# Making the down projection's input factors on chip, from raw activations, instead of reading them ready-made from DRAM

## The chip, the cores and the metric

One Trainium2 chip, and one of its cores: TensorE (PE) multiplies 128x128 tiles, VectorE (DVE) and ScalarE (ACT) do elementwise work, GpSimd (POOL) a little of it, and SyncE (SP) issues the transfers between DRAM and the on-chip memory SBUF, which 16 DMA engines carry out. The metric is the time of one execution on the device in microseconds (us), the median of several runs.

## The reference

One layer of an encoder over 2048 positions with a width of 1024: a mixer of three head groups, and then a gated feed-forward network (FFN) with a convolution, each within normalisations, conditioned scales and a residual. Only the FFN matters here:

```
h  = rms_norm(x, g_pre_ffn) * (1 + sc_f) + sh_f
up = dwconv3(h @ w_up, conv_w, conv_b)         # w_up: 1024 x 5632, width-3 convolution over positions
gate, val = split(up, 2)
y  = (gelu(gate) * val) @ w_down               # w_down: 2816 x 1024
x  = x + gt_f * rms_norm(y, g_post_ffn)
```

All of it is float32.

## The kernel before

Channels lie on the 128 partitions and positions along the free dimension. Every large product is computed in float16 with a float32 sum: each operand is split into a high part (its float16 rounding) and a low part (the rest), and a product is three matmuls, high x high, low x high, high x low (`mm3`).

The two projections of the FFN also go by Strassen's scheme in Winograd's form: a product of two matrices of 2 x 2 blocks takes seven products of blocks and not eight, and each of the seven multiplies a sum or a difference of blocks, a *factor*, by another. The kernel numbers them 1 to 7. For the down projection the blocks of the activations are two neighbouring k-tiles of 128 channels (a = 2j, b = 2j + 1) by two halves of 512 positions; with b11, b12 the two halves of a, and b21, b22 those of b, the activation factors are: 1: b11; 5: t5 = b12 - b11; 6: t6 = b22 - t5; 3: b22; 7: b22 - b12; 2: b21; 4: b21 - t6. The weights have factors of their own, made in SBUF by `wcomb` and written to DRAM (`wdd`) by `down_weights` during the up projection.

The positions are worked through in two *halves* (`p` in the up projection, `nt` in the down projection): 0 is positions 0 to 1022 after the convolution and 1 the rest. The down projection wants 1024 positions in each, so position 1023 comes from `p` = 1: it is the last column of a 512 column block in half 0, and the column is kept in `self.gx`.

*Up projection* (`ffn`): for each half, 22 pairs of tiles (a gate and a value), each with seven products; `up_act` convolves, applies the gelu and multiplies, and writes the result, float32, to DRAM (`grd`). Both halves of the up projection come before the down projection.

*Factors* (`gcomb`, lines 1785 to 1815): one process for each half, and in each, eleven pairs j of k-tiles. It loads the two raw tiles (2 x 512 KB), makes four combinations with four subtractions on VectorE (`tt`, line 277), splits all of it in high (ScalarE, `act`, line 272) and low (VectorE, line 277), and stores seven factors of 256 KB to DRAM (`gd`). The one for half 0 follows the up projection of half 1, pair by pair (`f_up[1][2j]`). The one for half 1 follows the down projection of half 0: it waits for `f_down[j]`, which is set at every third step of that. Column 511 is left out in half 0; `gx_comb` makes it for all factors (`gxc`) when the last pair of the up projection is done.

*Down projection* (`down`, from line 1865): for each half, products in the order `ORDER` = 1, 5, 6, 3, 7, 2, 4, and for each six steps k of two pairs j (the sixth has one). A step is 4 output tiles x 2 pairs x 3 = 24 matmuls of 512 columns, and a product 132. In half 0 the first product is computed for 511 columns, and then for the one column from `gxc` with 132 further matmuls. `down_stream` (line 1845) feeds it: for each step it loads a tile of weight factors and a tile of activation factors, 512 KB each, up to `D_LEAD` = 7 steps ahead. `down_evac` brings a product's four PSUM banks to the output tiles Y and sums their squares; when an output half is complete, after product 7 and after product 4, `ffn_out` normalises it, adds the residual and stores it. Its normalisation needs a small float32 matmul with ones on TensorE.

*The order of the work.* Processes are Python generators. Each yields the engine it wants, a planned duration and an earliest time, and a planner (`Sched`) with its own clock for each engine takes the request that can start first, with priorities among equals; the order that results, and for each instruction its planned start as a priority, goes to the framework, which puts every engine's instructions into one fixed list, allots the tiles and sets the waits. At run time each engine goes through its list in order, so an instruction that waits holds up all that stands behind it on its engine. All transfers are issued on SP's queue (`dma`, line 267). A transfer of n bytes is planned as n / 340e3 us of the queue and 2 us until it has landed; an addition of n columns on VectorE as 0.07 + 0.00105 n, a copy on ScalarE as 0.2 + 0.00084 n, and each hands on 0.12 us later.

SBUF's working tiles are 50 slots of 4112 bytes a partition (`u`): a 512 KB tile of weights, of factors or of raw activations takes one.

Of the kernel before, what the change touches and what calls it, by code (L numbers as in the profile page):

```python
# [10 lines left out]
F16 = mybir.dt.float16  # L11
I32 = mybir.dt.int32
AF = mybir.ActivationFunctionType
ALU = mybir.AluOpType
# [57 lines left out]
W_LEAD, W_RAW, U_PAIRS, D_LEAD, TAIL = 3, 1, 4, 7, 2  # L72
# [130 lines left out]
class Builder:  # L203
# [1452 lines left out]
    def ffn(self):  # L1656
        A = self.A
        self.cwt, self.carry = self.const([P, 44, 4]), self.const([P, 44, 2])
        self.gx, self.gxc = self.const([P, 2, NFF]), self.const([P, 7, 11, 2], F16)
        self.gd, self.wdd = self.dt([7, 2, 11, P, 1024], F16), self.dt([7, 11, P, 1024], F16)  # L1660
# [4 lines left out]
        self.f_g = [[Fut() for _ in range(11)] for _ in range(2)]  # L1665
        self.f_gr, self.f_down = [[Fut() for _ in range(NFF)] for _ in range(2)], [Fut() for _ in range(11)]
        self.grd = self.dt([2, NFF, P, 1024], F32)
        for p in range(2):
            self.sc.spawn(self.gcomb(p), 4)
        self.f_up = [[Fut() for _ in range(NFF)] for _ in range(2)]  # L1670
        self.f_gx, self.f_wd = Fut(), [Fut() for _ in range(11)]
# [74 lines left out]
    def up_act(self, p, i, U, f, done, pairs):  # L1746
# [32 lines left out]
        if p and i == NFF - 1:  # L1779
            self.sc.spawn(self.gx_comb(t + 0.3))  # L1780
# [3 lines left out]

    def gcomb(self, p):


        n, v = 511 + p, lambda x: x.rearrange("p (a b) -> p a b", a=2)
        e = G_ADD
        for j in range(11):  # L1790
            if p == 0:
                t = yield ("w", self.f_up[1][2 * j])
            else:
                t = yield ("w", self.f_down[j])
            for i in (2 * j, 2 * j + 1):
                yield ("w", self.f_gr[p][i])
            a, b = self.u([2, n]), self.u([2, n])
            ta = yield from self.dma(max(t, self.f_gr[p][2 * j].t), a, v(self.grd[p, 2 * j, :, 0:2 * n]))
            tb = yield from self.dma(max(t, self.f_gr[p][2 * j + 1].t), b, v(self.grd[p, 2 * j + 1, :, 0:2 * n]))
            t12, t34 = self.u([2, n]), self.u([2, n])  # L1800
            o = [self.u([2, 2, 512], F16) for _ in range(4)]
            if p == 0:
                for x in o:
                    yield from self.mset(0, x[:, :, :, 511:512], 0.0, eng="G")
            t1 = yield from self.tt(ta, t12[:, 0], a[:, 1], a[:, 0], ALU.subtract, eng=e[0])
            t3 = yield from self.tt(max(ta, tb), t34[:, 0], b[:, 1], a[:, 1], ALU.subtract, eng=e[1])
            t2 = yield from self.tt(max(t1, tb), t12[:, 1], b[:, 1], t12[:, 0], ALU.subtract, eng=e[2])
            t4 = yield from self.tt(t2, t34[:, 1], b[:, 0], t12[:, 1], ALU.subtract, eng=e[3])
            w = 0.0
            for i, (t, src, rs) in enumerate(((ta, a[:, 0], (1,)), (tb, b, (2, 3)), (t2, t12, (5, 6)),  # L1810
                                              (max(t3, t4), t34, (7, 4)))):
                t = yield from self.split(t, o[i][:, :, :, 0:n], src)
                for c, r in enumerate(rs):
                    w = yield from self.dma(t, self.gd[r - 1, p, j].rearrange("p (x n) -> p x n", x=2), o[i][:, :, c])
            self.f_g[p][j].set(w)

    def gx_comb(self, t):

        v = self.gx.rearrange("p s (j a) -> p a s j", a=2)
        (b12, b11), (b22, b21) = [(v[:, a, 0], v[:, a, 1]) for a in range(2)]  # L1820
        d = self.const([P, 4, 11], name="gt")
        S = ALU.subtract
        t = yield from self.tt(t, d[:, 0], b12, b11, S)
        t = yield from self.tt(t, d[:, 1], b22, d[:, 0], S)
        t = yield from self.tt(t, d[:, 2], b22, b12, S)
        t = yield from self.tt(t, d[:, 3], b21, d[:, 1], S)
        for r, src in ((1, b11), (2, b21), (3, b22), (4, d[:, 3]), (5, d[:, 0]), (6, d[:, 1]), (7, d[:, 2])):
            hi, lo = self.gxc[:, r - 1, :, HI], self.gxc[:, r - 1, :, LO]
            t = yield from self.act(t, hi, src, AF.Copy)
            t = yield from self.tt(t, lo, src, hi, S)  # L1830
        self.f_gx.set(t)
# [13 lines left out]
    def down_stream(self, q, lead):  # L1845
        for nt in range(2):
            for r in self.ORDER:
                for k in range(6):
                    t = yield ("acq", lead, 1)
                    n = 2 if k < 5 else 1  # L1850
                    for j in range(2 * k, 2 * k + n):
                        t = max(t, (yield ("w", self.f_wd[j])), (yield ("w", self.f_g[nt][j])))
                    w, g = self.u([n, 2, 512], F16), self.u([n, 2, 512], F16)
                    v = lambda d: d[2 * k:2 * k + n].rearrange("j p (x n) -> p j x n", x=2)
                    yield from self.dma(t, w, v(self.wdd[r - 1]))
                    t = yield from self.dma(t, g, v(self.gd[r - 1, nt]))
                    if nt == 0 and r != self.ORDER[0]:
# [7 lines left out]
    def down(self):  # L1865
# [6 lines left out]
        for nt in range(2):  # L1872
# [6 lines left out]
            for r in self.ORDER:  # L1879
# [19 lines left out]
                for pi, (c0, c1) in enumerate(parts):  # L1899
# [3 lines left out]
                    for k in range(6):  # L1903
# [13 lines left out]
                        if wide == 512 and pi == len(parts) - 1:  # L1917
                            lead.give(t)
# [229 lines left out]
```

## Time and profile before

| | us |
|---|---|
| median of 3 runs | 2234.53 (2234.34 to 2235.89) |
| the profiled execution's own time | 2235.86 |
| its span, first to last instruction | 2234.1 |
| TensorE busy, in the span | 2004.5 (90%) |
| VectorE busy | 1596.0 (71%) |
| ScalarE busy | 984.2 (44%) |
| GpSimd busy | 266.9 (12%) |

Over the span the DMA engines moved 478.11 MB, 214 GB/s in the mean. In the trace, times are counted from the span's start. TensorE's busy time comes from modelled ends of pipelined matmuls, so the count of matmuls in a stretch is the surer measure of its speed. "Granted clock" is the share of TensorE's full clock that the throttle left it. A row of a group of instructions has: line, engine, operation, out<-in (`u` a slot, `c` a constant, `ps` a PSUM bank, `d` DRAM), shapes, count | busy us, mean ns of one | idle time of the engine just before them and what ended it. A row of the timeline has: start, length, engine, line, operation, names, shapes, count, and in brackets the idle time before.

### The profile page before, as it was taken

What the parts mean: (1) busy time and instruction counts of PE and PEld (TensorE: products, weight loads), DVE (VectorE), ACT (ScalarE), POOL (GpSimd) and SP (SyncE); (2) the same over time, 40 slices, a digit from 0 to 9 for tenths busy, and PEclk for the clock granted to TensorE, in tenths of its full rate; (3) what the DMA queues carried; (4) which work ended last, traced back from release to release, by engine and by line L of the source; (5) the groups of instructions that cost most, each with busy time, mean ns of one, the idle gap of its engine ahead of it and who ended that gap; (6) DMA issues with size and microseconds to landing.
All of it is one profiled execution on the core that took longest, in us unless ns stands there. A gap on an engine that the chain in (4) does not pass through costs nothing.

```text
span 2234.1 us, 28331 instructions
## 1 busy us (share of the span) xinstructions
PE 2004.5 (90%) x10252; PEld 1000.6 (45%) x10252; DVE 1596.0 (71%) x2455; ACT 984.2 (44%) x1657; POOL 266.9 (12%) x390
## 2 busy tenths in 40 slices
PE   6778777989998778998999999999999999975997
PEld 2335565545554335443444444444444444432445
DVE  8999999976665665889988875878887724362016
ACT  3623232436566665566655543555555422211001
POOL 0564554020000000000000000000000000020002
PEclk9899899999999888999999999999999999997999
DMA  9351134772825453336655557888887899989933
GB/s 368 110 175 60 44 104 148 250 252 67 287 100 150 138 191 103 127 128 254 235 190 195 186 207 274 286 296 295 281 297 265 291 323 336 346 285 320 375 110 108
DMA packets 263919, 478.11 MB, mean 214 GB/s; under 512 B 23266, under 2 KB 149475, under 8 KB 263779
## 3 DMA queue, kind: packets, MB, share of 16 engines
q1 hardware_dynamic: 263778, 476.31, 61.4%
q8 instruction: 80, 1.31, 0.2%
q14 instruction: 61, 0.49, 0.1%
HBM read 299.30 MB, written 175.35 MB: 212 GB/s over the span
## 4 chain that ended last, share of the span: by engine, by line
PE 58%; DVE 26%; ACT 5%; issue 4%; DMA 4%; SPq 2%; POOL 1%; DVEq 0%; POOLq 0%; ACTq 0%
PE ps L318 58%; DVE u L277 13%; DVE u L291 9%; ACT u L272 5%; DMA u<-d 2%; DVE u L302 2%; SPq L267 2%; DVE u L446 1%; POOL u L277 1%; DVE u L284 0%; DMA u<-w_up 0%; DVE u L410 0%; DVE u L1327 0%; DMA u<-x 0%; DMA u<-w_ada 0%
## 5 line engine op out<-in xcount | busy, mean ns | idle before, releaser
L318 PE MATMUL ps<-u,u 128*128 128x512 f16 (+10 forms) x9306 | 1917.5, 365 | 158.4 <-DMA u<-d 53.1
L318 PEld LDWEIGHTS <-u 128*128 128x128 f16 (+1 forms) x9466 | 875.1, 101 | 1075.4 <-issue 178.4
L272 ACT ACTIVATE u<-u 128x1024 f16<-128x1024 f32 (+10 forms) x487 | 405.1, 861 | 378.2 <-DMA u<-d 126.1
L277 DVE TENSOR_TENSOR u<-u,u 128x512 f32<-128x512 f32 (+10 forms) x618 | 502.5, 845 | 74.4 <-ACT u L272 37.2
L272 ACT ACTIVATE u<-ps 128x512 f32<-128x512 f32 (+6 forms) x511 | 276.0, 555 | 536.8 <-PE ps L318 514.9
L291 DVE SCALAR_TENSOR_TENSOR u<-ps,u 128x512 f32<-128x512 f32 (+3 forms) x231 | 151.9, 664 | 264.5 <-PE ps L318 227.5
L291 DVE SCALAR_TENSOR_TENSOR u<-u,c,u 128x1023 f32<-128x1023 f32 (+5 forms) x248 | 293.5, 1203 | 46.1 <-ACT u L272 42.0
L291 DVE SCALAR_TENSOR_TENSOR u<-u,u 128x1024 f16<-128x1024 f32 (+7 forms) x225 | 239.7, 1090 | 24.0 <-ACT u L272 21.7
L277 POOL TENSOR_TENSOR u<-u,u 128x288 f32<-128x288 f32 (+9 forms) x169 | 189.2, 1134 | 420.5 <-DVE u L291 255.9
L277 DVE TENSOR_TENSOR u<-u 128x512 f32<-128x512 f32 (+8 forms) x206 | 106.0, 525 | 118.5 <-DMA u<-d 75.0
L272 ACT ACTIVATE u<-u,c 128x1023 f32<-128x1023 f32 (+2 forms) x104 | 120.0, 1157 | 108.8 <-DVE u L291 102.9
L307 POOL MEMSET u<- 128x1 f32 (+1 forms) x132 | 13.4, 104 | 1156.9 <-PE ps L318 615.8
L272 ACT ACTIVATE u<-u,st 128x384 f32<-128x384 f32 (+3 forms) x192 | 108.7, 594 | 35.8 <-DVE st L284 20.1
L318 PEld LDWEIGHTS ps<-u,u 128*128 128x128 f32 (+1 forms) x532 | 93.7, 189 | 65.2 <-DVE u L277 36.5
L318 PE MATMUL ps<-u,c 128*128 128x32 f32 (+4 forms) x190 | 66.3, 456 | 40.2 <-DVE u L302 18.0
L318 PE MATMUL ps<-c,u 128*128 128x128 f16 (+2 forms) x700 | 65.2, 217 | 17.9 <-ACT u L272 11.4
L272 ACT ACTIVATE c<-u 128x2 f32<-128x2 f32 (+1 forms) x88 | 17.8, 202 | 124.6 <-DVE u L291 124.4
L1327 DVE CUSTOM_DVE_ANT_0 u<-ps,u 128x384 f32<-128x384 f32 (+1 forms) x96 | 49.2, 537 | 29.9 <-PE ps L318 29.2
L302 DVE TENSOR_TENSOR_SCAN u<-u,u 128x512 f32<-128x512 f32 (+1 forms) x72 | 68.8, 963 | 1.1 <-ACT u L272 0.9
L291 DVE SCALAR_TENSOR_TENSOR u<-u,st,u 128x384 f16<-128x384 f32 (+1 forms) x96 | 55.6, 607 | 11.9 <-ACT u L272 11.6
L318 PEld LDWEIGHTS ps<-u,c 128*128 128x128 f32 (+1 forms) x190 | 29.1, 176 | 73.1 <-issue 29.1
L277 DVE TENSOR_TENSOR u<-ps,u 128x512 f32<-128x512 f32 (+2 forms) x96 | 56.1, 603 | 5.6 <-PE ps L318 5.2
(58 smaller groups left out, 379.9 us busy)
## 6 DMA issues: line engine op xcount, KB each, us to landing
u<-d SPq DMA_DIRECT2D x298, 512.0 KB
d<-u SPq DMA_DIRECT2D x158, 512.0 KB
d<-u SPq DMA_DIRECT2D x265, 256.0 KB
u<-w_ada SPq DMA_DIRECT2D x48, 512.0 KB
u<-w_up SPq DMA_DIRECT2D x44, 512.0 KB
u<-d SPq DMA_DIRECT2D x76, 256.0 KB
u<-x SPq DMA_DIRECT2D x32, 512.0 KB
u<-d SPq DMA_DIRECT2D x26, 511.0 KB
```

Of the source, the lines that this page charges most:

```text
L267: self.SP.dma_start(out, in_)
L272: self.S.activation(out, in_, func, **kw)
L277: (self.V if eng == "V" else self.G).tensor_tensor(out, a, b, op)
L291: self.V.scalar_tensor_tensor(out, a, s, b, op0, op1)
L302: self.V.tensor_tensor_scan(out, d0, d1, 0.0, ALU.mult, ALU.add)
L307: (self.V if eng == "V" else self.G).memset(out, v)
L318: self.PE.matmul(o, a, b, start=st, stop=sp, skip_group_check=chain)
L446: V.tensor_tensor_reduce(out=w, in0=w, in1=self.crep, op0=ALU.mult, op1=ALU.add, scale=1.0, scalar=0.0, accum_out=mod[:, j:j + 1])
L1327: V.tensor_tensor_reduce(out=s_, in0=o, in1=self.bias[h // 2][:, h % 2, bo:bo + nk * 128], op0=ALU.add, op1=ALU.max, scale=1.0, scalar=-3e ...
```

## The change

`gcomb` and `gx_comb` are taken out, and with them the factors in DRAM (`gd`) and the column constants (`gxc`). `down_stream` now loads raw activations and makes the factors itself. In products 1, 5, 6 and 2 each step loads one raw block of two pairs, float32, 512 KB, into a slot (`load`: X1 = b11, X2 = b12, X3 = b22, X4 = b21); in half 0 the block has 511 columns from DRAM and its last by a small ScalarE copy out of `self.gx`. The combination is made in place by one subtraction over both pairs: product 5 turns X1 into X2 - X1, product 6 that into X3 - X1, product 7 turns X2 into X3 - X2, product 4 turns X1 into X4 - X1; products 3 and 2 take X3 and X4 as they are. So X1 lives from product 1 to product 4, X2 from 5 to 7, X3 from 6 to 7, X4 from 2 to 4. Then each step splits its factor in high (ScalarE) and low (VectorE). The first product of half 0 has all 512 columns, the one-column matmuls are gone, and `D_LEAD` is 6. The order of the seven products in `ORDER` stays as it was, and so do the weights' factors.

```diff
--- before.py
+++ after.py
@@ -69,7 +69,7 @@
 W_ON_V = 2
 N_SL = 3
 W_ADD, H_ADD, G_ADD, SSQ = "VVVV", "V", "VVVV", "V"
-W_LEAD, W_RAW, U_PAIRS, D_LEAD, TAIL = 3, 1, 4, 7, 2
+W_LEAD, W_RAW, U_PAIRS, D_LEAD, TAIL = 3, 1, 4, 6, 2
 F_GATE, H_GATE, D_FROM = 1, 1, (1, 0, 2)
 N_CH = 3
 N_PE = (1,)
@@ -1656,19 +1656,15 @@
     def ffn(self):
         A = self.A
         self.cwt, self.carry = self.const([P, 44, 4]), self.const([P, 44, 2])
-        self.gx, self.gxc = self.const([P, 2, NFF]), self.const([P, 7, 11, 2], F16)
-        self.gd, self.wdd = self.dt([7, 2, 11, P, 1024], F16), self.dt([7, 11, P, 1024], F16)
+        self.gx, self.wdd = self.const([P, 2, NFF]), self.dt([7, 11, P, 1024], F16)
         yield from self.dma(0, self.cwt, A["cw"])
         yield ("w", self.f_pc[F_GATE])
         wq, lead = [Fut() for _ in range(2 * NFF)], Sem(W_LEAD)
         self.sc.spawn(self.up_weights(wq, lead, Sem(W_RAW)))
-        self.f_g = [[Fut() for _ in range(11)] for _ in range(2)]
-        self.f_gr, self.f_down = [[Fut() for _ in range(NFF)] for _ in range(2)], [Fut() for _ in range(11)]
+        self.f_gr = [[Fut() for _ in range(NFF)] for _ in range(2)]
         self.grd = self.dt([2, NFF, P, 1024], F32)
-        for p in range(2):
-            self.sc.spawn(self.gcomb(p), 4)
         self.f_up = [[Fut() for _ in range(NFF)] for _ in range(2)]
-        self.f_gx, self.f_wd = Fut(), [Fut() for _ in range(11)]
+        self.f_wd = [Fut() for _ in range(11)]
         self.sc.spawn(self.down_weights(), 4)
         pairs = Sem(U_PAIRS)
         for p in range(2):
@@ -1776,59 +1772,9 @@
         t = yield from self.stt(max(t, tms[1]), g, g, SA, c[1][:, :NT], ALU.mult, ALU.mult)
         x = 1022 if p == 0 else 0
         yield from self.act(t, self.gx[:, p, i:i + 1], g[:, x:x + 1], AF.Copy)
-        if p and i == NFF - 1:
-            self.sc.spawn(self.gx_comb(t + 0.3))
         t = yield from self.dma(t, self.grd[p, i, :, 0:1022 + 2 * p], c[0][:, p:p + 1022 + 2 * p])
         pairs.give(t)
         done.set(t)
-    def gcomb(self, p):
...
-    def gx_comb(self, t):
...
 
     def down_weights(self):
@@ -1843,24 +1789,60 @@
     ORDER = (1, 5, 6, 3, 7, 2, 4)
 
     def down_stream(self, q, lead):
+        S = ALU.subtract
         for nt in range(2):
+            n = 511 + nt
+            X = {}
+            def load(x, k, ab, half):
+                i0, m = 4 * k + ab, 2 if k < 5 else 1
+                z = self.u([m, 512])
+                X[x, k] = z
+                t = 0.0
+                for i in range(i0, i0 + 2 * m, 2):
+                    for p in range(2):
+                        t = max(t, (yield ("w", self.f_gr[p][i])))
+                t = yield from self.dma(t, z[:, :, 0:n], self.grd[nt, i0:i0 + 2 * m - 1:2, :, half * n:half * n + n]
+                                        .rearrange("i p n -> p i n"))
+                if nt == 0:
+                    t1 = yield from self.act(0, z[:, :, 511], self.gx[:, 1 - half, i0:i0 + 2 * m - 1:2], AF.Copy)
+                    t = max(t, t1)
+                return t
             for r in self.ORDER:
                 for k in range(6):
                     t = yield ("acq", lead, 1)
-                    n = 2 if k < 5 else 1
-                    for j in range(2 * k, 2 * k + n):
-                        t = max(t, (yield ("w", self.f_wd[j])), (yield ("w", self.f_g[nt][j])))
-                    w, g = self.u([n, 2, 512], F16), self.u([n, 2, 512], F16)
-                    v = lambda d: d[2 * k:2 * k + n].rearrange("j p (x n) -> p j x n", x=2)
-                    yield from self.dma(t, w, v(self.wdd[r - 1]))
-                    t = yield from self.dma(t, g, v(self.gd[r - 1, nt]))
-                    if nt == 0 and r != self.ORDER[0]:
-                        t0 = yield ("w", self.f_gx)
-                        t = yield ("G", 0.15, max(t, t0))
-                        self.G.tensor_copy(g[:, :, :, 511], self.gxc[:, r - 1, 2 * k:2 * k + n, :])
-                        t += self.LAT
+                    m = 2 if k < 5 else 1
+                    w, g = self.u([m, 2, 512], F16), self.u([m, 2, 512], F16)
+                    for j in range(2 * k, 2 * k + m):
+                        t = max(t, (yield ("w", self.f_wd[j])))
+                    tw = yield from self.dma(t, w, self.wdd[r - 1, 2 * k:2 * k + m].rearrange("j p (x n) -> p j x n", x=2))
+                    if r == 1:
+                        t, x = (yield from load(1, k, 0, 0)), X[1, k]
+                    elif r == 5:
+                        t, x = (yield from load(2, k, 0, 1)), X[1, k]
+                        t = yield from self.tt(t, x, X[2, k], x, S)
+                    elif r == 6:
+                        t, x = (yield from load(3, k, 1, 1)), X[1, k]
+                        t = yield from self.tt(t, x, X[3, k], x, S)
+                    elif r == 3:
+                        x = X[3, k]
+                    elif r == 7:
+                        x = X[2, k]
+                        t = yield from self.tt(t, x, X.pop((3, k)), x, S)
+                    elif r == 2:
+                        X.pop((2, k))
+                        t, x = (yield from load(4, k, 1, 0)), X[4, k]
+                    else:
+                        x = X.pop((1, k))
+                        t = yield from self.tt(t, x, X.pop((4, k)), x, S)
+                    t = yield from self.act(t, g[:, :, HI], x, AF.Copy)
+                    t = yield from self.tt(t, g[:, :, LO], x, g[:, :, HI], S)
                     f = next(q)
-                    f.set(t, (w, g))
+                    f.set(max(t, tw), (w, g))
 
     def down(self):
         futs = [Fut() for _ in range(84)]
@@ -1893,9 +1875,8 @@
                     for mp in range(4):
                         t = max(t, (yield ("w", fe[{3: 5, 6: 1, 7: 6, 4: 7}[r], mp])))
                 first = r in (1, 5, 2)
-                wide = 511 if nt == 0 and r == self.ORDER[0] else 512
                 un = []
-                parts = [(0, 308), (308, 512)] if last else [(0, wide)]
+                parts = [(0, 308), (308, 512)] if last else [(0, 512)]
                 for pi, (c0, c1) in enumerate(parts):
                     if pi:
                         for mp in range(4):
@@ -1914,29 +1895,14 @@
                                 t = yield from self.mm3(max(t, ff.t), banks[mp][:, c0:c1], (w[:, j, HI, sl], w[:, j, LO, sl]),
                                                         (g[:, j, HI, c0:c1], g[:, j, LO, c0:c1]), first and k == 0 and j == 0,
                                                         k == 5 and j == n - 1, r != 2)
-                        if wide == 512 and pi == len(parts) - 1:
-                            lead.give(t)
-                        x = 6 * self.ORDER.index(r) + k
-                        if nt == 0 and x % 3 == 0 and x < 33:
-                            self.f_down[x // 3].set(t)
-                    if wide == 511:
-                        tg = yield ("w", self.f_gx)
-                        for k in range(6):
-                            w, _ = un[k].val
-                            for mp in range(4):
-                                sl = slice(mp * P, mp * P + P)
-                                for j in range(2 if k < 5 else 1):
-                                    x = self.gxc[:, r - 1, 2 * k + j]
-                                    t = yield from self.mm3(max(t, tg), banks[mp][:, 511:512],
-                                                            (w[:, j, HI, sl], w[:, j, LO, sl]), (x[:, HI:HI + 1], x[:, LO:LO + 1]),
-                                                            False, k == 5, True)
+                        if pi == len(parts) - 1:
                             lead.give(t)
                     m0, half, copy = plan[r]
                     final = r in (3, 7, 2, 4)
                     for mp in range(4):
                         e = fe[r, mp] = Fut()
                         free = r in (3, 2, 4) and pi == len(parts) - 1
-                        s = slice(c0, c1 if wide == 512 else 512)
+                        s = slice(c0, c1)
                         prev = fin[half][-1] if final and fin[half] and pi == 0 else None
                         o = Fut()
                         self.sc.spawn(self.down_evac(t, banks[mp], s, Y[m0 + mp][:, half], copy, free, e,
```

More of the change, by code (lines that the diff above doesn't have):

```diff
@@ L1783, in up_act @@
         done.set(t)
-    def gcomb(self, p):
[L1788 to L1815, printed above, removed]
@@ L1817, in gx_comb @@
-    def gx_comb(self, t):
[L1819 to L1831, printed above, removed]
```

## The prediction

> **What bounds the kernel now.** I first read the page's shares, then the busy time of stretches of the FFN, then TensorE's instructions and waits from the start of the down projection on, then the queue that issues the transfers. In the table of stretches the columns are: from:to, its length, busy us (count) of PE, PEld, DVE, ACT, POOL, granted clock, DMA share, GB/s.
>
> ```profile
> span 2234.1 us, 28331 instructions
> 1650.00:1700.00 50.00, 50.00 (x234) 22.65 (x232) 43.57 (x48) 30.07 (x43) 1.46 (x14) 1.00 0.87 297
> 2000.00:2020.00 20.00, 5.61 (x21) 2.13 (x19) 7.99 (x10) 4.99 (x6) 0.00 (x0) 0.67 0.70 227
> 2020.00:2040.00 20.00, 6.94 (x24) 2.84 (x25) 9.12 (x11) 4.07 (x5) 0.00 (x0) 0.60 0.91 298
> 2060.00:2080.00 20.00, 20.00 (x94) 9.10 (x93) 0.00 (x0) 2.39 (x4) 0.00 (x0) 1.00 1.05 388
> ```
>
> At 1650 us, in the second half of the up projection, TensorE is busy for all 50 us although VectorE works 43.6 of them and the transfers 0.87 of the time: whatever is taken off those two there gains nothing. At 2060 the down projection runs at 94 matmuls in 20 us, 0.213 us each. So a step of the stream (two k-tiles, 24 matmuls) is 5.11 us, a product (132 matmuls) 28.1. Between 2000 and 2040 TensorE works 12.6 of 40 us. Its instructions in order of time, with the idle time ahead of each group, show where:
>
> ```profile
> 1759.81 4.26 PE L318 MATMUL ps<-u,u 128*128 128x512 f16 x19
> 1767.74 31.41 PE L318 MATMUL ps<-u,u 128*128 128x511 f16 x132 [3.67 <-DMA u<-d]
> 1798.98 3.44 PE L318 MATMUL ps<-c,u 128*128 128x1 f16 x132
> 1998.56 7.05 PE L318 MATMUL ps<-u,u 128*128 128x512 f16 x24 [7.88 <-DMA u<-d]
> 2032.91 6.94 PE L318 MATMUL ps<-u,u 128*128 128x512 f16 x24 [27.30 <-DMA u<-d]
> 2042.12 18.25 PE L318 MATMUL ps<-u,u 128*128 128x512 f16 x76 [2.27 <-DMA u<-d]
> PE ps L318 <- DMA u<-d: 41.1, 4, 27.3
> ```
>
> The last row is from the table of waits from 1760 us on: four waits for a load from DRAM, 41.1 us, are all of TensorE's idle time on transfers in the down projection. One lies at its start, three (7.88 + 27.30 + 2.27 = 37.45 us) where the second half begins. Each of these three stands ahead of one step of the stream: the loads of factors for k-tiles 6 and 7, 8 and 9, 10. What the issuing queue did meanwhile:
>
> ```profile
> 2019.16 0.55 SPq L267 DMA_DIRECT2D u<-d  x1
> 2020.28 4.37 SPq L267 DMA_DIRECT2D d<-u  x6
> 2024.70 2.02 SPq L267 DMA_DIRECT2D u<-d  x3
> 2032.14 0.53 SPq L267 DMA_DIRECT2D d<-u  x1
> 2032.71 0.61 SPq L267 DMA_DIRECT2D u<-d  x1
> 2033.88 3.91 SPq L267 DMA_DIRECT2D d<-u  x6
> 2037.83 7.36 SPq L267 DMA_DIRECT2D u<-d  x11
> ```
>
> This is `gcomb(1)`: a k-tile's raw activations come in (2019, 2024), VectorE and ScalarE make factors, seven stores of 256 KB go out (one and six), and only behind them the load TensorE waits for. TensorE runs on 4.3 us after the load at 2037.83. The bound of this stretch is that round trip through DRAM in one in-order queue.
>
> **Removed.** `gcomb` of both halves, `gx_comb`, the 132 one-column matmuls, and every load of a factor.
> (a) The three waits. The second half's raw blocks have lain in DRAM since the up projection, so their loads wait for a free slot alone. Gain 37.45 us.
> (b) The slow clock behind them. The 48 matmuls after the first two waits took 7.05 + 6.94 = 13.99 us against 48 x 0.213 = 10.2, and the 76 after the third 18.25 against 16.2: 5.9 us, at a granted clock of 0.60 to 0.67. Gain 5.9.
> (c) The one-column matmuls lie on TensorE's own path: 3.44 us. The 132 matmuls ahead of them get one column more, nothing that a row can show.
> (d) `gcomb(0)` works under a TensorE that is busy all the time (row 1650): 0.
>
> **Added or moved.** The durations, of the down projection's own groups and of ScalarE's first convolution of the last pair:
>
> ```profile
> L277 DVE TENSOR_TENSOR u<-u,u 128x1024 f16<-128x1024 f32 x33 | 38.7, 1217 | 7.1 <-ACT u L272 7.1
> L277 DVE TENSOR_TENSOR u<-u,u 128x512 f32<-128x512 f32 x55 | 38.6, 725 | 30.4 <-DMA u<-d 21.1 <-ACT u L272 8.6
> L291 DVE SCALAR_TENSOR_TENSOR u<-u,c,u 128x512 f32<-128x512 f32 x16 | 16.4, 1058 | 0.1
> L291 DVE SCALAR_TENSOR_TENSOR u<-ps,u 128x512 f32<-128x512 f32 x14 | 9.3, 688 | 13.1 <-PE ps L318 8.7 <-ACT u L272 4.4
> L272 ACT ACTIVATE u<-u 128x1024 f16<-128x1024 f32 x35 | 36.3, 1052 | 23.1 <-DMA u<-d 17.4 <-DVE u L277 5.2
> 1763.39 1.24 ACT L272 ACTIVATE u<-u,c 128x1025 f32<-128x1025 f32 x1 [6.49 <-DVE u L291]
> ```
>
> A step now makes its own factor: a copy on ScalarE (1.05), a subtraction for the low part on VectorE (1.22) and, in products 5, 6, 7 and 4, one more subtraction over 1024 float32 columns. No row has that shape; it lies between 1.22, as the low part of the same width, and two of 512, 1.45. I take 1.22, the row of the same width. So a step asks 1.2 to 2.4 us of VectorE and 1.05 of ScalarE under 5.11 of TensorE. Over a half VectorE does 7 x 5.5 x 1.22 + 4 x 5.5 x 1.22 = 74 us where `gcomb` did 11 x (4 x 0.73 + 3.5 x 1.22) = 79: the work stays, the first half's moves from the up projection into 198 us of TensorE's products. It costs nothing while steps run ahead. What covers it is the lead of six steps, 30 us, against a chain of load (4.3), subtraction (1.2), copy (1.05), low part (1.2), under 8 us without queueing. Two extra steps of queueing still leave it covered; with a lead of one step it would cost 8 - 5.1, some 3 us a step.
>
> Transfers: a half of the down projection loads 38.5 weight tiles of 0.5 MB as before, and 22 raw ones of that size in place of 38.5 of factors; with residual and output (8 MB) about 40 MB in 198 us, 200 GB/s, against 388 in row 2060. On the queue 24 issues replace 42 loads, 22 loads and 77 stores. `D_LEAD` 6 for 7 costs nothing while the chain is under 30 us. In the first half each raw tile's last column comes by a ScalarE copy of two elements; ScalarE may stand behind the tile's landing there, with the evacuations that copy queued behind it. Those have a whole product (28 us) until their bank is wanted again, so 0.
>
> (e) The start. Now the first factor is loaded ready-made. TensorE ends the up projection at 1764.07 and waits 3.67 us, because of this order in the queue and on the chain of waits:
>
> ```profile
> 1756.42 0.61 SPq L267 DMA_DIRECT2D u<-d  x1
> 1757.13 6.23 SPq L267 DMA_DIRECT2D d<-u  x6
> 1763.41 4.37 SPq L267 DMA_DIRECT2D u<-d  x7
> 1763.41 4.29 DMA u<-d
> ```
>
> The first weight tile is issued at 1756.42; the factor stands behind six stores of `gcomb(0)`. These go, so the raw tile can be issued about 1757 and land about 1761. Then its copy and low part queue among the last pair's `up_act`, whose first convolution on ScalarE starts at 1763.39. Best case: the factor is ready before 1764.07, and the 3.67 us are gained. Worst case: it stands behind the whole `up_act` of the last pair, whose last VectorE work ends about 1773.7 in
>
> ```profile
> 1764.67 1.29 DVE L291 SCALAR_TENSOR_TENSOR u<-u,c,u 128x1025 f32<-128x1025 f32 x1 [1.02 <-ACT u L272]
> 1772.50 1.23 DVE L291 SCALAR_TENSOR_TENSOR u<-u,u 128x1025 f32<-128x1025 f32 x1
> ```
>
> and then 1.05 + 1.22 more: a wait of 12 us, 8.3 worse. The planner that writes the order gives the chain 7.5 us from the end of the last product (two loads of 1.54, 2.0 to land, a copy of 1.06, a subtraction of 1.15, three times 0.12); the early issue takes about two of these back. I take a wait of 5.7, a loss of 2 us. The cold clock stays: the 132 matmuls behind 3.67 us of waiting took 31.41 us against 28.1, 3.3 lost, as I expect again.
>
> The Trainium skill, "TensorE: Matmul & The Clock Gate", Part 1, says that the array falls to half rate after an idle window of about 3.4 us. By that rule a start with a shorter wait would be warm, and the sum below would be smaller by those 3.3 us and the shorter wait. The trace agrees that a gap just over 3.4 us was paid for.
>
> **Sum.** The profiled execution took 2235.86 us (span 2234.1 and 1.8 around it), 1.3 above the median of the runs, 2234.53. 2235.9 - 37.5 - 5.9 - 3.4 + 2.0 = 2191.1 on that scale, 1.3 less on the median's: 2190.
>
> **Rivals.**
> A. VectorE becomes late where it also finishes a half. In the product behind product 7, and in the one behind product 4 of the first half, it has the steps' 13.6 us (5.5 x 2 x 1.22), `ffn_out`'s 8 x 1.06 + 4 x 0.73 = 11.4, evacuation 2.8, sums of squares 2.9: 30.7 us under 28.1. In its in-order queue it also stands still for the norm (8.62 and 4.43 us at the first half's end):
>
> ```profile
> 1975.43 3.08 DVE L277 TENSOR_TENSOR u<-u,u 128x512 f32<-128x512 f32 x4 [8.62 <-ACT u L272]
> 1982.95 0.69 DVE L291 SCALAR_TENSOR_TENSOR u<-ps,u 128x512 f32<-128x512 f32 x1 [4.43 <-ACT u L272]
> ```
>
> Together some 16 us behind, which a lead of six steps covers and one of two (10 us) doesn't: 6 us at each of three places, 18 in all, 2208 (2198 to 2220). Against it: `gcomb(1)` put as much on VectorE in the first half, and TensorE waited for nothing but loads there.
>
> B. Slots run out, and it is slower. The pool has 50: three sets of raw blocks are 18, six steps 12, the half's output and sums 10, and at the change of halves the old outputs are another 10 and the residual 4. From 50 live on the loads wait for a release, and the lead falls to a step. Each step of products 5 and 6 then pays the chain, 7.8 - 5.1 = 2.7 us and the wait for its slot; 22 such steps in the two halves are 59 us, 2249. It decides from a lead of one step. For it: 18 slots for raw blocks are new. Against: I count 40 to 42 live in each stretch, since the old outputs go within a product.
>
> C. The three waits are not `gcomb`'s but the queue's, behind output stores that wait for VectorE, and come back at the same place. Then only (c) is gained: 2231. Against it: the seven stores of factors stand directly ahead of each late load.
>
> **How the numbers follow.** Forecast 0.63, A 0.23, B 0.09, C 0.05. The forecast's own range is 2181 (no wait and a warm clock at the start: 5.7 + 3.3 less) to 2198 (the worst start). The range 2181 to 2216 takes in most of A and leaves out the rest of it, B and C. About 0.2% (4.5 us) is what a measurement tells from no change: C falls within it, B is slower, the rest faster: 0.86, 0.04, 0.10.
>
> **What would show it.** Right: TensorE's waits behind 1800 us add up to under 3 us; the first half's last product is followed by 94 matmuls in 20 us; no 128x1 matmuls; a wait of 3 to 8 us at the start, now ended by VectorE; DMA near 200 GB/s in the down projection. A would show as waits for VectorE one product behind products 7 and 4; B as queue waits for TensorE in products 5 and 6 and a TensorE wait in each step. I am wrong if a wait of over 10 us stands at the change of halves, or if the up projection's 1650 row loses its full 50 us.

## The result and the profile after

The changed kernel takes 2199.5 us (median of four runs, 2196.1 to 2203.7) where the kernel before takes 2235.2 (2234.3 to 2238.6). The ratio is 0.9838, with a 95% interval of 0.9816 to 0.9860: 1.6% faster, 36 us. The forecast was 2190 from 2234.5, 45 us. The profiled execution is the longest of the four, 2203.73 us, 32.1 less than the profiled one of before.

The first view of it is the span, then TensorE's waits from 1740 us on (total, times, longest), then its instructions in order of time, as they were shown of the kernel before.

```profile
span 2202.0 us, 27575 instructions
...
PE ps L318 <- ACT u L272: 8.7, 2, 4.4
PE ps L318 <- DVE u L277: 5.7, 3, 3.5
...
1754.81 12.68 PE L318 MATMUL ps<-u,u 128*128 128x512 f16 x58
1771.78 1.44 PE L318 MATMUL ps<-u,u 128*128 128x512 f16 x3 [4.29 <-ACT u L272]
1773.47 178.02 PE L318 MATMUL ps<-u,u 128*128 128x512 f16 x816 [0.24 <-DVE u L277]
1951.32 1.02 PE L318 MATMUL ps<-u,c 128*128 128x512 f32 x2
...
1979.45 8.83 PE L318 MATMUL ps<-u,u 128*128 128x512 f16 x27 [4.44 <-ACT u L272]
...
2177.94 0.79 PE L318 MATMUL ps<-u,c 128*128 128x308 f32 x2 [1.89 <-DVE u L277]
2178.56 8.04 PE L318 MATMUL ps<-u,u 128*128 128x204 f16 x90
2190.14 1.05 PE L318 MATMUL ps<-u,c 128*128 128x204 f32 x2 [3.54 <-DVE u L277]
```

The waits for loads from DRAM, 41.1 us before, are gone, and so are the 128x1 matmuls. In their place stand a wait of 4.29 + 0.24 us at the start, now for the factor made on ScalarE and VectorE (3.67 before, for its load), and two that were not there: 4.44 us at the change of halves, for ScalarE, and 1.89 us for the last normalisation. The 3.54 us at the very end were there before. The table of stretches, with the columns of the prediction:

```profile
1650.00:1700.00 50.00, 50.00 (x234) 22.62 (x233) 35.30 (x39) 22.64 (x34) 0.49 (x5) 1.00 0.62 211
1960.00:1980.00 20.00, 15.56 (x72) 6.93 (x71) 11.30 (x12) 3.20 (x5) 4.61 (x3) 0.96 0.80 251
1980.00:2000.00 20.00, 20.00 (x81) 8.44 (x79) 13.63 (x18) 5.85 (x10) 3.20 (x2) 0.87 0.62 203
2060.00:2080.00 20.00, 20.00 (x94) 9.06 (x93) 8.29 (x8) 8.77 (x12) 0.00 (x0) 1.00 0.58 182
```

In the up projection VectorE has 8.3 us of 50 less to do and the transfers carry 211 GB/s for 297; TensorE was busy all 50 us and still is. In the down projection TensorE goes at its 94 matmuls in 20 us, and of the stretches behind its start only 1960 to 2000 shows a loss: the wait, and 81 matmuls in the 20 us behind it.

Where does that wait come from? TensorE wants a PSUM bank there: the second half's first product goes into the banks that product 4 of the first half leaves, and ScalarE empties them. ScalarE's list at that time, from its timeline:

```profile
1952.87 2.51 ACT L272 ACTIVATE u<-u 128x1024 f16<-128x1024 f32 x3
1968.02 1.06 ACT L272 ACTIVATE u<-u 128x1024 f16<-128x1024 f32 x1 [12.64 <-DMA u<-d]
1977.86 1.06 ACT L272 ACTIVATE u<-u 128x1024 f16<-128x1024 f32 x1 [8.78 <-DMA u<-d]
1978.82 1.07 ACT L272 ACTIVATE u<-ps 128x512 f32<-128x512 f32 x2
```

The rows `128x1024 f16` are the copies for the second half's first factors, the row `u<-ps` is the evacuation. The evacuation stands behind two copies, and these wait for raw blocks that have not landed. And SP's queue, its timeline from 1880 us, with the kind of wait that is its longest one (46.0 us in all from 1880 to 1985, 30.6 the longest):

```profile
1880.94 46.98 SPq L267 DMA_DIRECT2D u<-d  x18
1959.71 3.31 SPq L267 DMA_DIRECT2D out<-u  x2
1963.08 0.46 SPq L267 DMA_DIRECT2D u<-d  x1
1965.59 4.51 SPq L267 DMA_DIRECT2D out<-u  x2
1970.19 19.65 SPq L267 DMA_DIRECT2D u<-d  x16
...
SPq L267 <- DVE u L277: 46.0, 10, 30.6
```

SP issues nothing from 1928 to 1959.7: the next entry of its list is an output store of the block that product 7 completed, which waits 30.6 us for VectorE, and the raw loads of the second half are listed between and behind the four output stores. VectorE had little to do meanwhile: its timeline has it idle for 14.49 us ahead of 1943.75 and for 5.09 ahead of 1953.95. What the store waits for is the normalisation of its block, whose matmul with ones is listed on TensorE at 1951.32 (the row `ps<-u,c` above), 159 matmuls or some 34 us behind the end of product 7. So the chain would be: output stores, raw loads, copies, evacuation, TensorE. That is theory 1 of the experiments; its rivals are that ScalarE or VectorE simply has too much to do there, and that the slots run out.

### The profile page after: what moved, and what is told of

Same layout as the page of the kernel before. It is cut to its first block, busy times and chain, and to the rows that moved or that the text cites. A ratio compares the mean times of both kernels' runs of the same rounds, so it can differ in the third digit from the quotient of the medians.

```text
span 2202.0 us, 27575 instructions
## 1 busy us (share of the span) xinstructions
PE 2004.0 (91%) x10120; PEld 1001.0 (45%) x10120; DVE 1597.4 (73%) x2400; ACT 984.3 (45%) x1670; POOL 246.6 (11%) x310
## 4 chain that ended last, share of the span: by engine, by line
PE 61%; DVE 25%; ACT 5%; issue 4%; DMA 3%; POOL 1%; SPq 1%; DVEq 0%; POOLq 0%; ACTq 0%
PE ps L318 61%; DVE u L277 12%; DVE u L291 8%; ACT u L272 5%; DVE u L302 2%; DVE u L446 1%; DMA u<-d 1%; POOL u L277 1%; SPq L267 1%; DMA u<-w_up 1%; DMA d<-u 1%; DVE u L284 0%; DVE u L410 0%; DMA u<-x 0%; DVE u L1327 0%
## 5 line engine op out<-in xcount | busy, mean ns | idle before, releaser
L318 PE MATMUL ps<-u,u 128*128 128x512 f16 (+9 forms) x9306 | 1918.7, 366 | 123.5 <-DVE u L277 35.7
L277 DVE TENSOR_TENSOR u<-u,u 128x512 f32<-128x512 f32 (+10 forms) x596 | 512.0, 892 | 107.0 <-ACT u L272 90.0
L272 ACT ACTIVATE u<-u 128x1024 f16<-128x1024 f32 (+8 forms) x483 | 403.2, 868 | 364.3 <-DVE u L277 158.8
L277 POOL TENSOR_TENSOR u<-u,u 128x288 f32<-128x288 f32 (+9 forms) x169 | 188.2, 1129 | 628.2 <-DVE u L291 459.1
L307 POOL MEMSET u<- 128x1 f32 x88 | 8.7, 99 | 1139.4 <-PE ps L318 510.9
L277 DVE TENSOR_TENSOR u<-u 128x512 f32<-128x512 f32 (+8 forms) x184 | 92.3, 513 | 23.6 <-ACT u L272 22.4
L318 PE MATMUL ps<-c,u 128*128 128x128 f16 (+1 forms) x568 | 61.9, 231 | 17.9 <-ACT u L272 11.4
L277 DVE TENSOR_TENSOR u<-ps,u 128x512 f32<-128x512 f32 (+2 forms) x96 | 56.0, 600 | 7.6 <-PE ps L318 6.9
```

What stands on the lines that cost most here:

```text
L272: self.S.activation(out, in_, func, **kw)
L277: (self.V if eng == "V" else self.G).tensor_tensor(out, a, b, op)
L307: (self.V if eng == "V" else self.G).memset(out, v)
L318: self.PE.matmul(o, a, b, start=st, stop=sp, skip_group_check=chain)
```

## The experiments

The kernel before was timed beside each; its median was 2235.7 to 2237.8 us in these comparisons, so ratios are compared and not microseconds. Each edit makes the planner write new lists, so it can move a little more than the lines that it names. In the diffs `<out>`, `<x>` and `<gd[...]>` stand for longer access patterns, and `...` for lines left out.

**e1: the output stores of one block on another queue.**

```diff
                 for c, w, p0 in runs:
-                    yield from self.dma(t, <out>, <x>)
+                    o = (<out>, <x>)
+                    if nt == 0 and half == 1:
+                        yield ("G", 0.1, t)
+                        self.G.dma_start(*o)
+                    else:
+                        yield from self.dma(t, *o)
```

> The changed kernel, but the four output stores of the first half's first finished block (after product 7) are issued on GpSimd's queue and not on SP's. Theory 1: the new 4.44 us wait of TensorE at the change of halves comes from SP's queue: it stands 30.6 us (1928 to 1959) at the first of these stores, so the raw loads of the second half's first product are late, their copies on ScalarE wait for them, and product 4's evacuations stand behind those copies. Then SP's long wait, the copies' wait for loads (12.6 and 8.8 us) and TensorE's 4.44 us go, with the slow clock behind it (3 us): 7 us less, about 2192. Rival 2, ScalarE or VectorE has too much to do there: TensorE's wait stays, 2199 as before. Rival 3, the slots have run out: SP waits for TensorE instead, 2199.

Measured: 2194.5 us, ratio 0.9811 (0.9794 to 0.9827), for the changed kernel's 0.9838. Its timelines, of TensorE, of ScalarE and of SP from 1900 us:

```profile
1953.79 27.36 PE L318 MATMUL ps<-u,u 128*128 128x512 f16 x126
1982.08 172.46 PE L318 MATMUL ps<-u,u 128*128 128x512 f16 x816
...
1954.48 4.41 ACT L272 ACTIVATE u<-u 128x1024 f16<-128x1024 f32 x5
1974.71 0.60 ACT L272 ACTIVATE u<-ps 128x512 f32<-128x512 f32 x1 [15.82 <-PE ps L318]
...
1900.68 59.22 SPq L267 DMA_DIRECT2D u<-d  x28
```

SP goes on with loads, five copies in a row find their data, ScalarE then waits for TensorE and not the other way round, and TensorE's 4.44 us are gone with the slow matmuls behind. SP's long wait has only moved: it now waits 27.2 us for VectorE at the output stores of the next block, up to 1988, and TensorE waits for nothing of that. Theory 1 holds; the copies and the evacuations are the same work on the same engines, so ScalarE's load is not the cause. The two intervals overlap; what settles it is the trace. In time it is 0.27%, 6 us, for the 7 expected.

**e2: a longer lead.** `D_LEAD` 8 for 6.

```diff
-W_LEAD, W_RAW, U_PAIRS, D_LEAD, TAIL = 3, 1, 4, 6, 2
+W_LEAD, W_RAW, U_PAIRS, D_LEAD, TAIL = 3, 1, 4, 8, 2
```

> The changed kernel with D_LEAD 8 in place of 6. Theory 1: two more steps of raw loads are put ahead of the output stores in SP's list, so the copies ahead of product 4's evacuations have their data: the 4.44 us wait goes or falls under 1 us, 2192 to 2195. Rival 3 (slots): 8 steps ask 4 more slots, so SP waits for TensorE more than the 149.6 us it does now, and waits of TensorE appear in products 5 and 6: over 2205. Rival 2 (ScalarE's or VectorE's work): no change, 2199.

Measured: 2199.5 us, ratio 0.9832 (0.9817 to 0.9846), no change that can be told. Its TensorE at the change of halves:

```profile
1979.90 8.97 PE L318 MATMUL ps<-u,u 128*128 128x512 f16 x33 [2.87 <-ACT u L272]
```

The wait fell to 2.87 us and not under 1. Four copies now find their data and not three, but six stand in front of the evacuation and not five, and the sixth still waits 5.45 us for a load behind the output stores. The expectation was wrong in its size, and by its time alone the run fits rival 2 as well; it is e1 that speaks against that one. That a longer lead asks too much of the slots did not come true either, since no wait of TensorE appears in products 5 and 6.

**e4: the kernel before, with the second half's factors asked for earlier** (`f_down[x // 2]` at every second step, for every third).

```diff
-                        if nt == 0 and x % 3 == 0 and x < 33:
-                            self.f_down[x // 3].set(t)
+                        if nt == 0 and x % 2 == 0 and x < 22:
+                            self.f_down[x // 2].set(t)
```

> The kernel before, but the factors of the second half are asked for earlier: pair j follows step 2j of the first half's down projection and not step 3j; nothing else. If the 37.5 us of waits were only a matter of starting late, the last pair is asked for 10 steps (51 us) earlier and the waits go: 2190 to 2200, as good as the change. If the round trip through one in-order queue is the limit (each pair's seven stores wait for VectorE in front of the loads, DMA 0.95 busy), the waits shrink little: 2220 to 2235. In between, it is both.

Measured: 2235.4 us, ratio 0.9994 (0.9982 to 1.0005). The waits are where they were:

```profile
2034.29 7.71 PE L318 MATMUL ps<-u,u 128*128 128x512 f16 x24 [26.94 <-DMA u<-d]
```

The experiment says less than was hoped. SP's list came out in the same order and at nearly the same times: its loads at 1990.2, 2011.7, 2020.7 and 2026.2 us stood at 1989.9, 2010.4, 2019.2 and 2024.7 before. So the edit moved the planner's request and not the transfers. The gate did not hold them; what did, this run doesn't show.

**b1 and b2: which stores hold the queue before.** In b1 the kernel before issues the first half's output stores on GpSimd's queue (the edit of e1, its condition `nt == 0` alone); in b2 the 77 stores of the second half's factors:

```diff
                 for c, r in enumerate(rs):
+                    if p:
+                        w = (yield ("G", 0.1, t)) + 2.8
+                        self.G.dma_start(<gd[r - 1, p, j]>, o[i][:, :, c])
+                        continue
                     w = yield from self.dma(t, <gd[r - 1, p, j]>, o[i][:, :, c])
```

> The kernel before, with the output stores of the first half issued on GpSimd's queue, and nothing else changed. Theory (the prediction's): the 37.5 us of waits are the round trip of the second half's factors, whose seven stores a pair stand in front of the loads: the waits shrink by less than 10 us, over 2226. Rival (the prediction's C, in part): the last three pairs' loads are late because the queue stands at output stores just as in the changed kernel: the waits shrink by more than 15 us, under 2220.

> The kernel before, with the 77 stores of the second half's factors issued on GpSimd's queue, and nothing else changed. Theory: SP's queue is no longer held by stores that wait for VectorE, and the loads of the next pairs and of the stream run ahead; the waits fall by more than 15 us, under 2220. Rival (output stores hold the queue): the loads of the last pairs still stand behind the output stores, the waits shrink by less than 10 us, over 2226. GpSimd's queue may itself be slow to issue them; then the waits grow and the trace shows it there.

b1 measured 2232.1 us, ratio 0.9986 (0.9976 to 0.9996); b2 2200.7, ratio 0.9836 (0.9821 to 0.9850). TensorE's waits for loads from 1740 us on, the start's among them, of b1:

```profile
PE ps L318 <- DMA u<-d: 37.4, 5, 28.9
```

and of b2, with the row of its transfers that counts the moved stores (the last figure is the median from issue to landing):

```profile
PE ps L318 <- DMA u<-d: 3.6, 1, 3.6
...
d<-u POOLq DMA_DIRECT2D x77, 256.0 KB, 7.1
```

b1 shrinks the waits by less than 10 us, as the theory said, but the time is 2232 and not under 2220; b2 comes out under 2220, as its theory said. So the output stores account for a tenth of the kernel's waits before (37.4 for 41.1 us), and the factor stores for all three at the change of halves: with them on another queue only the start's 3.6 us remain. The same 478 MB are moved, the same factors go through DRAM, and the kernel is as fast as the changed one. Two things leave SP with these stores. One is the waiting: between 1750 and 2050 us SP waited 92.0 us for VectorE's combinations and low parts (L277) before, and 21.1 in b2. The other is the issuing: 77 stores of 0.53 us or more, over 40 us. From 1785.6 to 1960 us SP now issues loads alone, 104 of them. b2 doesn't part the two.

**b3: all of these stores on GpSimd's queue**, of both halves' factors and of the first half's output, still in the kernel before.

```diff
                 for c, r in enumerate(rs):
+                    if True:
+                        w = (yield ("G", 0.1, t)) + 2.8
+                        self.G.dma_start(<gd[r - 1, p, j]>, o[i][:, :, c])
+                        continue
                     w = yield from self.dma(t, <gd[r - 1, p, j]>, o[i][:, :, c])
...
-                    yield from self.dma(t, <out>, <x>)
+                    o = (<out>, <x>)
+                    if nt == 0:
+                        yield ("G", 0.1, t)
+                        self.G.dma_start(*o)
+                    else:
+                        yield from self.dma(t, *o)
```

> The kernel before, with the factor stores of both halves and the first half's output stores issued on GpSimd's queue: the factors still go through DRAM, and the 132 one-column matmuls stay. If the gain of the change is the order in SP's queue and nothing else, this comes out as e6 (ratio 0.978) plus the one-column matmuls (3.4 us) and the 3.6 us wait with its slow clock at the start where that stays: 0.980 to 0.983, under the changed kernel's 0.9838. If the traffic of the factors through DRAM (81 MB more) costs something of its own, TensorE keeps waits for loads in the down projection's second half and the ratio stays above 0.984.

Measured: 2198.3 us, ratio 0.9827 (0.9811 to 0.9844). The first half of the down projection, and TensorE's waits for loads in all of it:

```profile
1800.00:1950.00 150.00, 146.24 (x675) 66.03 (x674) 75.32 (x98) 47.63 (x59) 58.85 (x99) 1.00 1.04 404
...
PE ps L318 <- DMA u<-d: 0.6, 1, 0.6
```

The time is in the range expected, but its interval reaches over 0.984, so it is the trace that decides. In these 150 us, with 404 GB/s of transfers, TensorE waits for no load at all; the 0.6 us of the last row are the start's wait, 0.55 us in place of 3.67. So the traffic through DRAM costs TensorE no wait for a load as long as no load stands behind these stores. It doesn't follow that the change itself is worth nothing: e6, below, has its stores on GpSimd's queue as well and comes out at 0.9767 to 0.9797, clear of b3. On the two profiled executions 5.9 us lie between them, of which the one-column matmuls are 3.4 and TensorE's waits from 1740 us on 2.4 (7.8 for 5.4).

**e5: the changed kernel, with the stream started one pair earlier** (`down_stream` is spawned ahead of the last pair's products, and not behind them).

```diff
+                if p == 1 and i == NFF - 1:
+                    self.d_futs, self.d_lead = [Fut() for _ in range(84)], Sem(D_LEAD)
+                    self.sc.spawn(self.down_stream(iter(self.d_futs), self.d_lead), 0)
...
-        futs = [Fut() for _ in range(84)]
-        lead = Sem(D_LEAD)
-        self.sc.spawn(self.down_stream(iter(futs), lead), 0)
-        q = iter(futs)
+        lead, q = self.d_lead, iter(self.d_futs)
```

> The changed kernel, but the stream of the down projection is started one pair earlier, ahead of the last pair's products of the up projection. Theory: the first factor is then ready when the up projection ends: TensorE's 4.29 + 0.24 us there go, and the clock stays up, which saves some 3.3 us more (5.2 us are lost in the first products of the changed kernel against 0.213 us a matmul): about 2191. Rival: the factors' copies and subtractions only take the place of the last pair's convolution on VectorE and ScalarE, whose result is then late somewhere else: 2196 to 2200.

Measured: 2193.2 us, ratio 0.9804 (0.9789 to 0.9818), against 0.9838 (0.9816 to 0.9860).

```profile
1754.65 189.45 PE L318 MATMUL ps<-u,u 128*128 128x512 f16 x877
...
1971.66 7.67 PE L318 MATMUL ps<-u,u 128*128 128x512 f16 x27 [4.05 <-ACT u L272]
```

TensorE goes from the up projection into the down projection without a stop. The other wait stays, 4.05 us: the two are separate.

**e6: both edits**, the early stream and all output stores of the first half on GpSimd's queue.

```diff
+                if p == 1 and i == NFF - 1:
...
+                    self.sc.spawn(self.down_stream(iter(self.d_futs), self.d_lead), 0)
...
+                    if nt == 0:
+                        yield ("G", 0.1, t)
+                        self.G.dma_start(*o)
```

> The changed kernel with both edits: the stream starts one pair earlier, and all output stores of the first half are issued on GpSimd's queue. If the two waits (4.5 us at the start, 4.4 at the change of halves) and the slow clock behind each are separate, their gains add: ratio to the kernel before 0.9838 - 0.0027 - 0.0034 = 0.978, about 2185 us where the kernel before takes 2235, and TensorE waits for nothing between the up projection and the last product. If one takes the place of the other, 0.980 as with one alone.

Measured: 2186.5 us (2186.1 to 2190.3), ratio 0.9782 (0.9767 to 0.9797): as expected, and the fastest version run. From 1740 us on TensorE waits 5.4 us, all of it for the last two normalisations:

```profile
PE ps L318 <- DVE u L277: 5.4, 2, 3.5
1749.73 192.47 PE L318 MATMUL ps<-u,u 128*128 128x512 f16 x891
```

**e7: 44 slots in place of 50.**

```diff
-    UNITS = 50
+    UNITS = 44
```

> The changed kernel with 44 slots in place of 50. If 40 to 42 slots are live in the down projection, as the prediction counted, TensorE's waits there stay as they are (4.5 at the start, 4.4 at the change of halves) within 2 us, and anything the total loses is lost ahead of the down projection. If the slots are used up (the prediction's rival B), waits of TensorE for its factors appear in products 5 and 6, 2.7 us a step: over 2215.

Measured: 2213.6 us, ratio 0.9895 (0.9880 to 0.9910).

```profile
1749.63 29.95 PE L318 MATMUL ps<-u,u 128*128 128x512 f16 x138
1783.92 1.44 PE L318 MATMUL ps<-u,u 128*128 128x512 f16 x3 [4.34 <-ACT u L272]
...
1991.14 7.50 PE L318 MATMUL ps<-u,u 128*128 128x512 f16 x27 [3.89 <-ACT u L272]
```

The up projection ends at 1779.6, 12 us later than with 50, so the stages ahead of the down projection want the slots. In the down projection the waits are the same ones, so 44 slots are enough there.

## Why the prediction was right, and where it was not

The direction and the mechanism were right; 2190 was forecast, and 9 us of the 45 did not come. That the range (2181 to 2216) holds the result is in part luck. The forecast's own part of it ended at 2198, and 2199.5 (or 2198.3, the ratio taken of the 2234.5 that the forecast starts from) lies at or over that edge, in the part that was put there for rival A, whose waits did not come. The edge was also set too high: the sum already holds 2.0 of the worst start's 8.3 us, so it is 2190 + 6.3 = 2196.

Other slips in the working change nothing: 5.5 x 2 x 1.22 is 13.4 and not 13.6, the planner's chain adds up to 7.65 and not 7.5, the "k-tiles 6 and 7, 8 and 9, 10" are pairs j, and the chances at the end, 0.86, 0.04 and 0.10, are not the 0.86, 0.09 and 0.05 that B and C would give.

Term by term, on the profiled executions:

(a) *The three waits, 37.45 us.* All gone, and b2 shows that their cause was the one named: the factor stores stand in front of the loads in one in-order queue. How much of it is their waiting for VectorE and how much their issuing stays open, as said at b2. What the prediction had too broadly is "round trip through DRAM": b2 and b3 keep the round trip and lose the waits. Rival C had a part of it, the tenth that b1 shows.

(b) *The slow clock behind them, 5.9 us.* Gone with them, but 3.1 us of it come back behind the new wait (27 matmuls in 8.83 us for 5.75).

(c) *The one-column matmuls, 3.44 us.* Gone.

(d) *`gcomb(0)`, 0.* Right; the row at 1650 us shows it.

(e) *The start, 2.0 lost.* 0.9: the wait is 4.5 us for the 5.7 taken. The first release was by ScalarE, and VectorE's low part, which the prediction named, came 0.24 us behind. e5 shows that the wait and the cold clock behind it were worth 0.34%, some 7.6 us, for the forecast 5.7 + 3.3.

*What the factors cost.* The subtraction of 1024 float32 columns, for which no row stood, took the 1.22 us that was chosen, the lower of the two ends:

```profile
L277 DVE TENSOR_TENSOR u<-u,u 128x1024 f32<-128x1024 f32 x40 | 47.9, 1220 | 15.4 <-ACT u L272 9.0 <-DMA u<-d 6.4
```

No wait of TensorE for a factor occurs once the stream runs, so the lead does cover the chain, as forecast.

*The step that failed* is the one that put ScalarE's copies behind a landing at nothing: "ScalarE may stand behind the tile's landing there, with the evacuations that copy queued behind it. Those have a whole product (28 us) until their bank is wanted again, so 0." It saw the mechanism, but for the small copies of the first half, and it took every bank to have a product's time. At the change of halves that does not hold: product 4's banks are wanted by the very next product. With e1 the runs show its cost, 4.44 us and 3.1 of slow clock, and its first cause, which the prediction counted among the queue's work without asking for whom it waits: the output stores, 30.6 us at the head of SP's list. Two of the prediction's signs of being right came out wrong by this. The first half's last product is followed by 81 matmuls in 20 us and not 94. And TensorE's waits behind 1800 us, which were to add up to under 3 us, come to 9.9 (4.44, 1.89 and 3.54); the 3.54 at the last normalisation stand in the kernel before too, so this sign was set too tight from the start.

Two smaller amounts complete the sum. The last normalisation's new wait is 1.89 us. And the up projection ended 3.4 us later than in the kernel before (1767.49 for 1764.07). This arose ahead of 1000 us, where the two kernels' work is the same: from 1000 to 1750 us TensorE runs 3408 matmuls before and 3410 after. In b2, whose source differs from the kernel before only in the down projection's stores, it ended at 1768.99, and in e4 at 1763.51, so this much varies between executions or schedules. Which of the two it is stays open. Together: -37.5 - 5.9 - 3.4 + 0.9 + 4.4 + 3.1 + 1.9 + 3.4 = -33.1, where -32.1 was measured.

*The rivals.* A named the place, but not the engine or the cause: VectorE was idle for part of that time and no step waited for it; ScalarE was held. B is refuted by e7 and e2: the down projection loses nothing with 44 slots, which fits the 40 to 42 counted. C was right on what an output store does to the queue, wrong on how much of the old waits it made.

The Trainium skill, "DMA: Bandwidth & Descriptors", section Rules for kernel authors, says that spreading transfers over the queues of SP, ACT and GpSimd doesn't help bandwidth, and only saves the sequencer's issue time. On bandwidth no run here decides. The second half is too narrow for these runs: the four stores that e1 moves take SP under 8 us in the changed kernel (the rows of 3.31 and 4.51), but they held the loads listed behind them for 30.6 us before that, because the first of them waited for its data.

## What to carry to other kernels

In a queue that issues in order, ask of each store what it waits for and which loads stand behind it; put stores that wait for an engine on a queue of their own before changing what is computed, for here that alone gave as much as the larger change (0.9836 for 0.9838), and the two kinds of edit together gave more (0.9782). When work moves onto an engine that also empties PSUM, look for the place where the next product wants the very bank just filled: there an operand that is late on that engine stops TensorE at once. And start a stream's first operands while the stage ahead still keeps TensorE busy: a wait of 4.5 us cost nearly twice that, with the slow clock behind it.

## What the runs showed of the hardware that was not expected

TensorE's clock suffered from a wait shorter than any that was priced: in e2, 2.87 us of waiting were followed by 33 matmuls in 8.97 us, 1.9 more than 33 x 0.213, at a granted clock of 0.91 in the 20 us from 1980. The Trainium skill, "TensorE: Matmul & The Clock Gate", Part 1, puts the loss behind an idle window of about 3.4 us; here less was enough. Nor does the length of a wait decide alone: in b2 a wait of 2.96 us at 1956 us was followed by 153 matmuls in 33.19 us, 0.6 more than 153 x 0.213, at a granted clock of 1.00. What sets the two cases apart no run here shows.

GpSimd's queue issued b2's 77 stores of 256 KB while VectorE was busy for half of the time (81.7 of the 165 us from 1790) and GpSimd copied its columns: 0.84 us each in the median to issue and 7.1 from issue to landing. All were issued by 1956 us, where the last went out at 2037.8 in the kernel before, and behind the start TensorE waited for no load. In b3 TensorE kept its 94 matmuls in 20 us beside 404 GB/s of transfers; the 3.8 us of waits in the 150 us shown there were for VectorE (2.5) and GpSimd (1.2).
